# Moving the activation rows of a float32 encoder from 64 to 112 bytes past a multiple of 256

## The chip, the cores and the metric

The kernel runs on one core of a Trainium2 chip. The metric is the device time of one execution in microseconds (us), and the number compared is the median of several executions. Before the change three executions took 1151.05, 1151.22 and 1156.51 us.

## What is computed

The reference is a trunk of two encoder layers over 256 tokens of width 1024, all in float32. One layer is

```
h = x + 0.5 * swiglu(rms_norm(x), w_ffn1_in, w_ffn1_out)          # 1024 -> 2*2816 -> 1024
q, k, v, c, g = split(rms_norm(h) @ w_in)                         # 512, 128, 128, 1024, 2048 columns
y_attn = window_attention(norm(q), norm(k), v, sink, bias) @ w_attn_out
y_conv = silu(layer_norm(depthwise_conv(glu(c)))) @ w_conv_out    # 31 taps, 512 channels
h = h + (sigmoid(g_attn) * y_attn + sigmoid(g_conv) * y_conv) @ w_o
h = h + 0.5 * swiglu(rms_norm(h), w_ffn2_in, w_ffn2_out)
x = h + (p @ w_pe_proj) * sigmoid(rms_norm(h) @ w_pe_gate)
```

Some 200 MB of weights are read once, and each weight is used for 256 tokens.

## The kernel before

**Layout.** Activations lie transposed: 128 channels on the partitions, and along a partition one row of 256 tokens (1024 bytes) for each group of 128 channels. A product with a weight matrix loads a 128x128 block of weights into TensorE (512 bytes per partition) and moves one such row of 256 tokens past it.

**Three products for one.** To keep float32 accuracy with the type float32r, every operand is cut in two: a high part, which is the value cast to float32r, and a low part, which is the rest. `mm3` (lines 309 to 317) then issues three matmuls for each 128x128 block: high weights on high rows (L315), high weights on low rows (L316), low weights on high rows (L317). Each matmul has a weight load of its own.

**Weights.** `Weights` (lines 42 to 135) loads units of 1 MB through the queue of SP (L76) into four raw buffers. From these ScalarE makes the high part (L100) and VectorE the low part (L101), in seven buffers each of `w_hi` and `w_lo`, 4096 bytes per partition. A unit is loaded once a raw buffer is free, and prepared some tiles ahead of its use.

**Stages of a layer.** `ffn` (L545) computes the 22 hidden groups (`ps_gu`), cuts each hidden row into `h_hi` and `h_lo`, and multiplies those down (`ps_fo`). `mix` (L593) computes the two halves of the convolution's input (`ps_c`), keys and values (`ps_kv`), queries (`ps_q`), the gates (`ps_g`), then attention, the output products in plain float32 (`ps_ao`, `ps_co`), and `w_o` on the rows `ym` (`ps_wo`). A second `ffn` follows, and `embed` (`ps_pp`, `ps_pe`). The order of instructions on each engine is set by a planner that goes by priorities and by the costs of its own model.

**Roles.** In `mm3` the weights are loaded and the rows move. In `keys_values` (L666, matmuls L676 to L678) and `queries` (L710, L720 to L722) it is the other way round: a 128-token piece of a row is loaded, and the prepared weights move, 256 columns at a time for the keys and values and 512 for the queries.

**Where the buffers lie.** Pools are laid one after another along each partition in the order in which they are opened, and a pool's tiles one after another in it. In the program before, the prepared weight tiles begin at byte 64768 and follow each other at steps of 4096 bytes, all multiples of 256. Behind them `gap0` at byte 122112, a tile of 64 bytes that nothing reads, moves what follows: `x32` at 122176, the rows' high part at 130368 and low part at 138560, which is 64 bytes past a multiple of 256 each. A second such gap (`gap1`) and one at the start of `mix_pool` do the same for `h_hi`, `h_lo`, `xe`, `pT` and `ym`. So every row that moves in `mm3` begins 64 bytes past a multiple of 256 and every block of weights at a multiple of 256. These addresses are those of the built program.

Of the kernel before, what the change touches and what calls it, by code (L numbers as in the profile page):

```python
# [9 lines left out]
F32 = mybir.dt.float32  # L10
F32R = mybir.dt.float32r
# [4 lines left out]
P = 128  # L16
T = 256
D = 1024
KD = D // P
L = 2  # L20
FF = 2816
KF = FF // P
# [3 lines left out]
KC = CD // P  # L26
# [10 lines left out]
WEIGHTS_LAG = 100  # L37
ATTN = 7
W_BUFS = 7


class Weights:
# [96 lines left out]
def encoder_kernel(ctx: ExitStack, tc: tile.TileContext, a: dict, out: bass.AP):  # L139
    nc = tc.nc  # L140
# [3 lines left out]
    raw_pool = ctx.enter_context(tc.tile_pool(name="raw_pool", bufs=RAW_BUFS))  # L144
    w_pool = ctx.enter_context(tc.tile_pool(name="w_pool", bufs=W_BUFS))
    gap0 = ctx.enter_context(tc.tile_pool(name="gap0", bufs=1))
    xp = ctx.enter_context(tc.tile_pool(name="xp", bufs=1))
    tmp = ctx.enter_context(tc.tile_pool(name="tmp", bufs=2))
    gap1 = ctx.enter_context(tc.tile_pool(name="gap1", bufs=1))
    edge = const.tile([P, 24], F32, name="edge")  # L150
    nc.gpsimd.memset(edge, 0.0)
    for gap in (gap0, gap1):
        nc.gpsimd.memset(gap.tile([P, 16], F32, name="gap"), 0.0)
    dram = ctx.enter_context(tc.tile_pool(name="dram", bufs=1, space=bass.MemoryType.DRAM))
    mmp = ctx.enter_context(tc.tile_pool(name="mmp", bufs=4, space=PS))
    atp = ctx.enter_context(tc.tile_pool(name="atp", bufs=2, space=PS))
# [4 lines left out]
    def at_tile(name):  # L161
        return atp.tile([P, 1024], F32, name=name, tag="at")
# [7 lines left out]
    for i in range(4):  # L170
        s = slice(i * 256, (i + 1) * 256)
# [5 lines left out]
    def load_params(tile_, rows, load):  # L177
        r0 = 0
        for name in rows:
            if name in ("q_norm", "k_norm"):  # L180
                for hf in range(2):
                    load(tile_[r0 : r0 + L, hf * HD : (hf + 1) * HD], a[name])
                r0 += L
                continue
            n = a[name].shape[1] // P
            load(tile_[r0 : r0 + L * n, :], a[name].rearrange("l (k p) -> (l k) p", p=P))
            r0 += L * n
# [150 lines left out]

    x32 = xp.tile([P, KD, T], F32, name="x32", tag="x32")

    def new_x(tag, name):
        return (
            xp.tile([P, KD, T], F32R, name=name + "h", tag=tag + "h"),
            xp.tile([P, KD, T], F32R, name=name + "l", tag=tag + "l"),
        )

    pending = []

# [94 lines left out]
    def bcast(r, n):  # L443
        return r.unsqueeze(1).broadcast_to([P, n, T])
# [38 lines left out]
    late = {}  # L483

    rows_late = ("norm_mix", "norm_ffn2", "norm_pe", "conv_b", "conv_ln_g", "conv_ln_b", "q_norm", "k_norm")

    def late_loads(hp):
        def load(dst, src):
            tc.keep_in_program_order(nc.sync.dma_start(dst, src))

        rows = hp.tile([80, P], F32, name="rows_late")
        load_params(rows, rows_late, load)
        cw_ld = hp.tile([TAPS * KC, L, P], F32, name="cw_ld")
        for l in range(L):
            load(cw_ld[:, l, :], a["conv_w"][l].rearrange("t (c p) -> (t c) p", p=P))
        onehot = hp.tile([33, NREL], F32, name="onehot")
        load(onehot, a["onehot"])
        rb = const.tile([33, NH], F32, name="rb")
        nc.gpsimd.memset(rb[32:33, :], NEG)
        load(rb[0:32, :], a["rel_bias"])  # L500
        sink = const.tile([P, L * NH], F32, name="sink")
        load(sink, a["sink"].rearrange("l h -> (l h)").partition_broadcast(P))
        late["sink"] = sink
        late["ld"] = rows, cw_ld, onehot, rb

    def late_params():
        place_params(late["ld"][0], rows_late, n_par)

    def late_tables(hp):
        rows, cw_ld, onehot, rb = late.pop("ld")  # L510
        cw = const.tile([P, L, TAPS, KC], F32, name="cw")
        for l in range(L):
            ps = at_tile("ps_cw")
            nc.tensor.transpose(ps[:, : TAPS * KC], cw_ld[:, l, :], ident[: TAPS * KC, : TAPS * KC])
            nc.scalar.copy(out=cw[:, l].rearrange("p t c -> p (t c)"), in_=ps[:, : TAPS * KC])
        late["cw"] = cw

        kg = const.tile([P, L], F32, name="kg")
        cq, ck = col["q_norm"][0], col["k_norm"][0]
        nc.vector.scalar_tensor_tensor(  # L520
            out=kg, in0=par[:, cq : cq + L], scalar=HD ** -0.5, in1=par[:, ck : ck + L], op0=ALU.mult, op1=ALU.mult
        )
        late["kg"] = kg

        ps = at_tile("ps_rb")
        nc.tensor.matmul(ps[:NH, :NREL], rb, onehot, start=True, stop=True)
        tb = hp.tile([NH, NREL], F32, name="tb")
        nc.vector.tensor_copy(tb, ps[:NH, :NREL])
        late["tb"] = tb
# [13 lines left out]


    def ffn(hp, l, x_in, stat_in, gain_name, xn, stat, hooks):  # L545
        h = (
            hp.tile([P, KF, T], F32R, name="h_hi"),
            hp.tile([P, KF, T], F32R, name="h_lo"),
        )

        def gate_up(j):
            ps, products = pair("ps_gu", x_in, j == 0)

            def evac():
                gu = tmp.tile([P, 2, T], F32, name="gu")
                nc.vector.tensor_tensor(
                    out=gu, in0=ps, in1=bcast(stat_in.r, 2), op=ALU.mult
                )
                sg = tmp.tile([P, T], F32, name="sg")
                nc.scalar.activation(out=sg, in_=gu[:, 0, :], func=AF.Silu)  # L560
                hh = tmp.tile([P, T], F32, name="hh")
                nc.vector.tensor_tensor(out=hh, in0=sg, in1=gu[:, 1, :], op=ALU.mult)
                split((h[0][:, j, :], h[1][:, j, :]), hh)

            group(products, evac)

        def down(f):
            ps = mm_tile("ps_fo")

            def evac():  # L570
                nc.vector.scalar_tensor_tensor(
                    out=x32[:, f, :], in0=ps[:, :T], scalar=0.5, in1=x32[:, f, :], op0=ALU.mult, op1=ALU.add
                )
                emit_x(f, pcol(gain_name, l, f), xn, stat)

            group(
                [
                    lambda i=i, k0=k0: mm3(ps[:, :T], ws.get(), h, first=i == 0, last=i == 2, x_k0=k0)
                    for i, (k0, n) in enumerate(KGROUPS)
                ],  # L580
                evac,
            )

        for j in range(KF):
            if j in hooks:
                hooks[j]()
            gate_up(j)
        for f in range(KD):
            down(f)
        flush_urgent()  # L590


    def mix(l, u, st, xn, stat):  # L593
        cw, kg, bias, sink = (late[n] for n in ("cw", "kg", "bias", "sink"))
        with tc.tile_pool(name="mix_pool", bufs=1) as mp:
            nc.gpsimd.memset(mp.tile([P, 8], F32, name="gap"), 0.0)
            cpad = mp.tile([P, KC, T + 2 * PAD], F32, name="cpad", tag="cpad")
            nc.gpsimd.memset(cpad[:, :, 0:PAD], 0.0)
            nc.gpsimd.memset(cpad[:, :, PAD + T :], 0.0)
# [302 lines left out]
            for i in range(KC):  # L902
# [5 lines left out]
                if i == 0:  # L908
# [1 line left out]

            ym = [
                (
                    mp.tile([P, KC, T], F32R, name=f"ym_h{i}", tag="s", bufs=2),
                    mp.tile([P, KC, T], F32R, name=f"ym_l{i}", tag="pTs", bufs=2),
                )
                for i in range(2)
            ]
# [104 lines left out]

    def embed_input(hp):
        p_ld = late.pop("p_ld")
        pT = (hp.tile([P, 2, T], F32R, name="pT_h"), hp.tile([P, 2, T], F32R, name="pT_l"))
        ps = mm_tile("ps_pt")
        for e in range(2):
            for t in range(2):
                nc.tensor.transpose(
                    ps[:, e * T + t * P : e * T + (t + 1) * P], p_ld[:, t, e * P : (e + 1) * P], ident  # L1030
                )
        split(pT, ps.rearrange("p (e t) -> p e t", e=2))
        late["pT"] = pT

    st = r_cur
    for l in range(L):
        with tc.tile_pool(name="ffn1_pool", bufs=1) as hp:
            hooks = {1: lambda: late_loads(hp), 5: late_params, 6: lambda: late_tables(hp), 8: late_write, 12: late_bias} if l == 0 else {}
            xn, stat = new_x("xa", f"xm{l}"), Stat()
            ffn(hp, l, x_cur, st, "norm_mix", xn, stat, hooks)  # L1040
        x_cur, st = xn, stat.finish(3, tokens=True)
        xn, stat = new_x("xa", f"xf{l}"), Stat()
        mix(l, x_cur, st, xn, stat)
        x_cur, st = xn, stat.finish(3)
        with tc.tile_pool(name="ffn2_pool", bufs=1) as hp:
            xe = (hp.tile([P, KD, T], F32R, name="xe_h"), hp.tile([P, KD, T], F32R, name="xe_l"))
            stat = Stat()
            ffn(hp, l, x_cur, st, "norm_pe", xe, stat, {0: lambda: embed_load(l), 4: lambda: embed_input(hp)})
            x_cur, st = xe, stat.finish(4)
            xn, stat = (new_x("xa", f"xn{l}") if l + 1 < L else None), Stat()  # L1050
            embed(l, x_cur, st, xn, stat)
            x_cur, st = xn, stat.finish(3)
# [39 lines left out]
```

## Time and profile before

| | |
|---|---|
| three executions | 1151.05, 1151.22, 1156.51 us |
| profiled execution, first to last instruction (span) | 1155.8 us |
| TensorE matmuls (PE) busy | 1136.7 us, 98% of the span |
| TensorE weight loads (PEld) busy | 1100.9 us, 95% |
| VectorE (DVE) busy | 812.1 us, 70% |
| ScalarE (ACT) busy | 610.4 us, 53% |
| DMA | 203 MB, 176 GB/s on average |

For the profiled execution the span is the only time there is; it lies 4.6 us above the median of the three and 0.7 us below the longest of them. A matmul's duration in the profile, some 280 ns, is not its cost: matmuls follow each other in a pipeline, and what one costs is the distance from its start to the start of the next.

### The profile page before, as it was taken

To read this page: it belongs to the slowest core of one execution; us is meant where nothing else is said; L and a number is where in the kernel's file an instruction comes from. 1 tells how busy PE (TensorE), PEld (TensorE's weight loads), DVE (VectorE), ACT (ScalarE), POOL (GpSimd) and SP (SyncE) were. 2 spreads that over 40 slices of the span, in tenths; PEclk is the share of its full clock that TensorE was granted. 3 is DMA by queue.
4 is the path that set the end of the run, shared out by engine and by line. 5 is a ranking of instruction groups with operands and counts; after the bars stand their busy time and mean duration, and the time that the engine had idled before them with its cause. 6 is when DMAs were issued, how large, how long until landed. Compare 5 with 4: busy or idle time off the path is not lost.

```text
span 1155.8 us, 21813 instructions
## 1 busy us (share of the span) xinstructions
PE 1136.7 (98%) x9082; PEld 1100.9 (95%) x9082; DVE 812.1 (70%) x1214; ACT 610.4 (53%) x1029; POOL 88.8 (8%) x123
## 2 busy tenths in 40 slices
PE   7999999999989999999999999999999999999998
PEld 7999999998879999999999999999987899999997
DVE  5866656798767766656886666669986686666564
ACT  6644444676346544444664444457753564444443
POOL 3000001211002000001110000113000010000110
PEclk9999999999999999999999999999999999999999
DMA  8866556545074565546556464566522664644541
GB/s 256 265 236 213 170 176 208 182 149 138 8 254 157 187 215 168 179 166 219 188 177 204 162 207 156 171 218 197 143 77 65 227 228 152 214 163 149 200 147 37
DMA packets 195695, 203.00 MB, mean 176 GB/s; under 512 B 3731, under 2 KB 188899, under 8 KB 195596
## 3 DMA queue, kind: packets, MB, share of 16 engines
q1 hardware_dynamic: 195564, 201.60, 52.9%
q8 instruction: 71, 1.16, 0.4%
q14 instruction: 28, 0.23, 0.1%
q10 hardware_dynamic: 32, 0.01, 0.0%
HBM read 200.53 MB, written 1.06 MB: 174 GB/s over the span
## 4 chain that ended last, share of the span: by engine, by line
PE 95%; DMA 2%; DVE 2%; ACT 1%; issue 0%; SPq 0%; ACTq 0%; DVEq 0%
PE ps_gu L317 14%; PE ps_gu L315 14%; PE ps_gu L316 14%; PE ps_fo L315 7%; PE ps_fo L317 7%; PE ps_fo L316 7%; PE ps_g L315 3%; PE ps_g L317 3%; PE ps_g L316 3%; PE ps_ao L852 2%; DMA raw<-in_w_o_dram 2%; PE ps_s L760 1%; PE ps_wo L316 1%; PE ps_c L315 1%; PE ps_pe L317 1%; PE ps_c L317 1%
## 5 line engine op out<-in xcount | busy, mean ns | idle before, releaser
L101 DVE TENSOR_TENSOR w_lo<-raw,w_hi 128x1024 fp32r<-128x1024 f32 (+1 forms) x368 | 441.6, 1204 | 227.8 <-ACT w_hi L100 225.9
L100 ACT CAST w_hi<-raw 128x1024 fp32r<-128x1024 f32 (+1 forms) x368 | 377.8, 1032 | 411.6 <-PE ps_gu L316 207.5
L315 PE MATMUL ps_fo<-h_hi,w_hi 128*128 128x256 f32 x704 | 196.1, 279 | 0.0
L316 PE MATMUL ps_fo<-h_lo,w_hi 128*128 128x256 f32 x704 | 195.9, 279 | 0.0
L317 PE MATMUL ps_fo<-h_hi,w_lo 128*128 128x256 f32 x704 | 195.9, 279 | 0.0
L317 PEld LDWEIGHTS ps_fo<-h_hi,w_lo 128*128 128x128 f32 x704 | 131.8, 188 | 0.0
L315 PEld LDWEIGHTS ps_fo<-h_hi,w_hi 128*128 128x128 f32 x704 | 131.8, 188 | 0.0
L316 PEld LDWEIGHTS ps_fo<-h_lo,w_hi 128*128 128x128 f32 x704 | 131.7, 187 | 0.0
L404 POOL TENSOR_TENSOR sq_acc<-sq_acc,sq 128x256 f32<-128x256 f32 x56 | 56.9, 1015 | 887.0 <-ACT sq L403 886.5
L315 PE MATMUL ps_gu<-x0h,w_hi 128*128 128x256 f32 x352 | 99.4, 282 | 2.0 <-ACT x L460 2.0
L612 DVE SCALAR_TENSOR_TENSOR y<-cpad,cw,y 128x256 f32<-128x256 f32 x240 | 101.2, 477 | 0.1
L317 PE MATMUL ps_gu<-x0h,w_lo 128*128 128x256 f32 x352 | 99.4, 282 | 0.2 <-DVE w_lo L101 0.2
L316 PE MATMUL ps_gu<-x0l,w_hi 128*128 128x256 f32 x352 | 98.9, 281 | 0.0
L315 PE MATMUL ps_gu<-xf0h,w_hi 128*128 128x256 f32 x352 | 98.6, 280 | 0.0
L315 PE MATMUL ps_gu<-xf1h,w_hi 128*128 128x256 f32 x352 | 98.6, 280 | 0.0
L316 PE MATMUL ps_gu<-xn0l,w_hi 128*128 128x256 f32 x352 | 98.5, 280 | 0.0
L315 PE MATMUL ps_gu<-xn0h,w_hi 128*128 128x256 f32 x352 | 98.4, 280 | 0.0
L316 PE MATMUL ps_gu<-xf0l,w_hi 128*128 128x256 f32 x352 | 98.4, 280 | 0.0
L316 PE MATMUL ps_gu<-xf1l,w_hi 128*128 128x256 f32 x352 | 98.4, 280 | 0.0
L317 PE MATMUL ps_gu<-xf0h,w_lo 128*128 128x256 f32 x352 | 98.3, 279 | 0.0
L317 PE MATMUL ps_gu<-xf1h,w_lo 128*128 128x256 f32 x352 | 98.3, 279 | 0.0
L317 PE MATMUL ps_gu<-xn0h,w_lo 128*128 128x256 f32 x352 | 98.2, 279 | 0.0
(225 smaller groups left out, 2677.8 us busy)
## 6 DMA issues: line engine op xcount, KB each, us to landing
raw<-in_w_ffn_in_dram SPq DMA_DIRECT2D x86, 1024.0 KB
raw<-in_w_in_dram SPq DMA_DIRECT2D x30, 1024.0 KB
raw<-in_w_ffn_out_dram SPq DMA_DIRECT2D x32, 896.0 KB
raw<-in_w_ffn_out_dram SPq DMA_DIRECT2D x16, 1024.0 KB
raw<-in_w_o_dram SPq DMA_DIRECT2D x8, 1024.0 KB
raw<-in_w_pe_gate_dram SPq DMA_DIRECT2D x8, 1024.0 KB
raw<-in_w_attn_out_dram SPq DMA_DIRECT2D x8, 512.0 KB
raw<-in_w_conv_out_dram SPq DMA_DIRECT2D x4, 1024.0 KB
```

Source lines behind the costliest of these rows:

```text
L100: nc.scalar.copy(out=hv[:, :, d0 : d0 + w], in_=src),
L101: nc.vector.tensor_tensor(out=lv[:, :, d0 : d0 + w], in0=src, in1=hv[:, :, d0 : d0 + w].bitcast(F32), op=ALU.subtract,),
L315: nc.tensor.matmul(ps, wh[:, k0 + k, cols], xh[:, kx, :], start=f, stop=False)
L316: nc.tensor.matmul(ps, wh[:, k0 + k, cols], xl[:, kx, :], start=False, stop=False)
L317: nc.tensor.matmul(ps, wl[:, k0 + k, cols], xh[:, kx, :], start=False, stop=e)
L404: nc.gpsimd.tensor_tensor(out=self.acc, in0=self.acc, in1=sq, op=ALU.add)
L612: nc.vector.scalar_tensor_tensor(out=y[:, i, :], in0=src, scalar=w, in1=y[:, i, :], op0=ALU.mult, op1=ALU.add)
L760: nc.tensor.matmul(ps[:, c, :], qT[v * HD : (v + 1) * HD, c, qb * P : (qb + 1) * P], kT[v * HD : (v + 1) * HD, :], start=True, stop=True,)
L852: nc.tensor.matmul(ps[:, c * T : (c + 1) * T], w[:, k, c * P : (c + 1) * P], x[:, k, :], start=k == 0, stop=k == KC - 1,)
```

## The change

The helper `rows` makes every pair of activation rows that `mm3` moves: the tile is 256 bytes longer (`ROW`, 64 elements), and the rows begin 16 bytes into it (`PLACE`, 4 elements). The gap ahead of the rows' pool grows from 64 to 96 bytes (`G0`); the other two keep their sizes. So `x`, `h`, `ym`, `xe` and `pT` begin at 96 + 16 = 112 bytes past a multiple of 256, and the other tiles behind the first gap (`x32`, scratch, the convolution's input and output, attention's tiles) move from 64 to 96 past it, the convolution's input from 96 to 128. The prepared weights stay where they were. A variable that was called `rows` is renamed.

```diff
+ROW = 64
+G0, G1, G2 = 24, 16, 8
+PLACE = 4
...
-    for gap in (gap0, gap1):
-        nc.gpsimd.memset(gap.tile([P, 16], F32, name="gap"), 0.0)
+    for gap, n in ((gap0, G0), (gap1, G1)):
+        nc.gpsimd.memset(gap.tile([P, n], F32, name="gap"), 0.0)
...
+    def rows(pool, k, name, **kw):
+
+        t = pool.tile([P, k * T + ROW], F32R, name=name, **kw)
+        return t[:, PLACE : PLACE + k * T].rearrange("p (k t) -> p k t", t=T)
+
     def new_x(tag, name):
-        return (
-            xp.tile([P, KD, T], F32R, name=name + "h", tag=tag + "h"),
-            xp.tile([P, KD, T], F32R, name=name + "l", tag=tag + "l"),
-        )
+        return tuple(rows(xp, KD, name + part, tag=tag + part) for part in "hl")
...
-        h = (
-            hp.tile([P, KF, T], F32R, name="h_hi"),
-            hp.tile([P, KF, T], F32R, name="h_lo"),
-        )
+        h = tuple(rows(hp, KF, "h_" + part) for part in ("hi", "lo"))
...
-            nc.gpsimd.memset(mp.tile([P, 8], F32, name="gap"), 0.0)
+            nc.gpsimd.memset(mp.tile([P, G2], F32, name="gap"), 0.0)
...
-                    mp.tile([P, KC, T], F32R, name=f"ym_h{i}", tag="s", bufs=2),
-                    mp.tile([P, KC, T], F32R, name=f"ym_l{i}", tag="pTs", bufs=2),
+                    rows(mp, KC, f"ym_h{i}", tag="s", bufs=2),
+                    rows(mp, KC, f"ym_l{i}", tag="pTs", bufs=2),
...
-        pT = (hp.tile([P, 2, T], F32R, name="pT_h"), hp.tile([P, 2, T], F32R, name="pT_l"))
+        pT = tuple(rows(hp, 2, "pT_" + part) for part in "hl")
...
-            xe = (hp.tile([P, KD, T], F32R, name="xe_h"), hp.tile([P, KD, T], F32R, name="xe_l"))
+            xe = tuple(rows(hp, KD, "xe_" + part) for part in "hl")
```

More of the change, by code (lines that the diff above doesn't have):

```diff
@@ L489, in load @@
             tc.keep_in_program_order(nc.sync.dma_start(dst, src))
-        rows = hp.tile([80, P], F32, name="rows_late")
-        load_params(rows, rows_late, load)
+        row_ld = hp.tile([80, P], F32, name="rows_late")
+        load_params(row_ld, rows_late, load)
         cw_ld = hp.tile([TAPS * KC, L, P], F32, name="cw_ld")
@@ L503, in late_loads @@
         late["sink"] = sink
-        late["ld"] = rows, cw_ld, onehot, rb
+        late["ld"] = row_ld, cw_ld, onehot, rb
     def late_params():
@@ L509, in late_tables @@
     def late_tables(hp):
-        rows, cw_ld, onehot, rb = late.pop("ld")
+        _, cw_ld, onehot, rb = late.pop("ld")
         cw = const.tile([P, L, TAPS, KC], F32, name="cw")
```

## The prediction

> **What bounds the kernel now.** I read the profile's page first: the busy shares, the granted clock, and the shares of the chain of waits by engine.
>
> ```profile
> span 1155.8 us, 21813 instructions
> ...
> PE 1136.7 (98%) x9082; PEld 1100.9 (95%) x9082; DVE 812.1 (70%) x1214; ACT 610.4 (53%) x1029; POOL 88.8 (8%) x123
> ...
> PEclk9999999999999999999999999999999999999999
> ...
> PE 95%; DMA 2%; DVE 2%; ACT 1%; issue 0%; SPq 0%; ACTq 0%; DVEq 0%
> ```
>
> TensorE has work in hand for 98% of the span, at the full clock in every slice, and 95% of the chain that ended last is TensorE itself. Then the list of what TensorE waited for, longest and shortest entry:
>
> ```profile
> PE ps_yc L893 <- DVE yn L883: 3.7, 2, 1.9
> ...
> PE ps_gu L317 <- DVE w_lo L101: 0.2, 1, 0.2
> ```
>
> No entry is above 3.7 us. So the end is set by how closely matmuls follow each other. The groups of instructions by line give their number; one row of each group stands for its three lines (L315, L316, L317), which have the same count:
>
> ```profile
> L315 PE MATMUL ps_fo<-h_hi,w_hi 128*128 128x256 f32 x704 | 196.1, 279 | 0.0
> L315 PE MATMUL ps_gu<-x0h,w_hi 128*128 128x256 f32 x352 | 99.4, 282 | 2.0 <-ACT x L460 2.0
> L315 PE MATMUL ps_g<-xm0h,w_hi 128*128 128x256 f32 x128 | 36.8, 287 | 0.0
> L315 PE MATMUL ps_pe<-xe_h,w_hi 128*128 128x256 f32 x128 | 36.5, 286 | 0.0
> L315 PE MATMUL ps_wo<-ym_h,w_hi 128*128 128x256 f32 x128 | 35.1, 282 | 0.5 <-ACT ym_h L448 0.5
> L315 PE MATMUL ps_c<-xm0h,w_hi 128*128 128x256 f32 x64 | 18.0, 282 | 0.0
> L315 PE MATMUL ps_pp<-pT_h,w_hi 128*128 128x256 f32 x32 | 8.9, 280 | 0.0
> ```
>
> `ps_gu` has four such groups (x0, xn0, xf0, xf1), `ps_g` and `ps_c` two each (xm0, xm1). That is 3 x (704 + 4 x 352 + 2 x 128 + 128 + 128 + 2 x 64 + 32) = 3 x 2784 = 8352 matmuls whose moved operand the change moves, out of 9082 records. What one costs, from start to start, comes from stretches inside an `ffn`, in which they run alone; the columns are the stretch, its length, PE busy with its count, clock, DMA share and GB/s:
>
> ```profile
> 420.00:520.00 100.00, 100.00 (x851) 1.00 0.52 173
> 980.00:1080.00 100.00, 100.00 (x851) 1.00 0.55 182
> ```
>
> 100 us / 851 = 117.5 ns each, in layer 0 and in layer 1 alike. 8352 x 117.5 ns = 981 us: 85% of the span.
>
> **Is that all the matmul needs?** The change can gain only if part of the 117.5 ns hangs on where operands lie. The trace of before holds rows of the same shape with another placement. For the keys and values the roles are exchanged: the loaded block is a piece of a row (64 bytes past a multiple of 256), the moved one is prepared weights (at the multiple). For the queries too, with 512 moved columns. Columns of these rows: count, shortest/median/longest duration in ns, first to last start.
>
> ```profile
> L676 PEld LDWEIGHTS ps_kv<-w_hi,xm0h x16: 187/188/188, 213.9 to 219.0; 128*128 128x128 f32 x16
> L676 PE MATMUL ps_kv<-w_hi,xm0h x16: 276/276/283, 214.0 to 219.1; 128*128 128x256 f32 x16
> ...
> L676 PE MATMUL ps_kv<-w_hi,xm1h x16: 276/276/282, 780.7 to 785.8; 128*128 128x256 f32 x16
> ```
>
> ```profile
> L720 PE MATMUL ps_q<-w_hi,xm0h x16: 388/396/398, 219.5 to 230.0; 128*128 128x512 f32 x16
> L720 PE MATMUL ps_q<-w_hi,xm1h x16: 388/396/398, 786.2 to 796.7; 128*128 128x512 f32 x16
> ```
>
> Each line here is every third matmul, so from the first start to the last lie 15 x 3 = 45 distances. Keys and values: 5.1 us / 45 = 113.3 ns, in both layers. The same 128x128 load, the same 256 moved columns, the same type, 4.2 ns less; what differs is which operand lies 64 bytes on. Queries: 10.5 us / 45 = 233.3 ns for twice the columns. Two bounds for a stream that nothing disturbs come from the chain of waits in order of time (start, us, what): plain float32 matmuls, and transposes, which pass 128 columns at half speed.
>
> ```profile
> 273.72 0.87 PE ps_pt L797 x8
> ...
> 313.23 2.59 PE ps_ao L852 x12
> ```
>
> 0.87 us / 8 = 108.8 ns; 2.59 / 12 = 215.8 ns, which is twice 107.9. In time these stand for 256 and 512 columns at full speed. So a matmul of `mm3` runs 8.7 ns above the closest spacing that the trace shows for such a stream, one of the keys 4.5 ns above it, one of the queries 233.3 - 215.8 = 17.5 ns. I read this as two readers of the same memory, the moved rows and the next weight load, that get in each other's way by an amount that depends on their relative place. That is an inference: no row shows a collision itself.
>
> A rule of the Trainium skill speaks against it: "TensorE: Matmul & The Clock Gate", section "Step-by-step: what each phase is for", says that TensorE has two independent read ports to SBUF and that loading the next weights takes no bandwidth from the running matmul; by it the time would stay 1151 us. The rows of `ps_kv` and the 851-matmul stretches, 113.3 against 117.5 ns for one shape, do not fit that rule as it stands, though they don't show the cause.
>
> **The change part by part.**
>
> 1. *The 8352 moved rows go from 64 to 112 bytes past the weights' place.* The trace of before has no row at 112. Bounds: below, 108.8 ns (nothing left to gain beyond it), which is 8352 x 8.7 ns = 73 us; above, the loss that one weight load causes in the queries, 108.8 + 17.5 = 126.3 ns, which is 8352 x 8.8 = 73 us more. Between ends so far apart I take the row that is nearest in shape, the keys' 113.3 ns: 8352 x 4.2 ns = 35 us less. In it the moved operand lies at -64, that is 192, from the loaded one; 112 is not there, but it too has left 64, and I have no reason to put it nearer to the worse side. "TensorE: Matmul & The Clock Gate" of the Trainium skill, section "Back-to-back issue gap", gives N/2.4 + 2.5 ns for a matmul by itself, which is 109.2 ns for 256 columns; the estimate by that page is 8352 x 8.3 ns = 69 us less.
>
> 2. *Keys, values and queries* now load at 112 and move at 0: 2 x 48 matmuls each. At worst they gain or lose what they stand above the bound, 96 x 4.5 + 96 x 17.5 ns = 2.1 us. I count 0. The plain float32 products (`ps_ao`, `ps_co`) already run at 215.8 ns, which is the bound, and their rows only move from 64 to 96: 0.
>
> 3. *ScalarE and VectorE write rows at 112 instead of 64.* The nearest rows: L627 writes the convolution's input 156 bytes past a multiple of 256, L449 writes rows at 64.
>
> ```profile
> L627 DVE TENSOR_TENSOR cpad<-sg,gu x8: 419/424/442, 217.0 to 815.4; 128x256 f32<-128x256 f32 x8
> ...
> L449 DVE TENSOR_TENSOR h_lo<-hh,h_hi x88: 417/419/427, 42.8 to 1062.2; 128x256 fp32r<-128x256 f32 x88
> ...
> L448 ACT CAST h_hi<-hh x88: 393/402/408, 41.6 to 1061.0; 128x256 fp32r<-128x256 f32 x88
> ```
>
> 424 against 419 ns: place costs VectorE at most 1%. For ScalarE there is no such row; were its casts (402 ns in the third row) twice as long, the 8 ends of stages at which TensorE may wait for the last row would each lose 0.4 us, 3 us in all. I take 0, since VectorE shows nothing.
>
> 4. *The longer tiles and the larger gap* cost one memset that clears 32 bytes more, and no instruction is added in any loop. The tiles fit: the second `ffn`'s pool ends 160 bytes below the partition's end. 0.
>
> **Does the supply keep up?** A faster TensorE asks sooner for weights. The stages (columns: stretch, length, then PE, PEld, DVE, ACT and POOL busy with counts, clock, DMA share, GB/s):
>
> ```profile
> 14.00:207.00 193.00, 192.97 (x1626) 191.86 (x1626) 128.86 (x158) 98.47 (x143) 14.33 (x17) 1.00 0.65 216
> ...
> 344.00:559.00 215.00, 215.00 (x1825) 214.89 (x1824) 145.06 (x182) 109.05 (x160) 14.43 (x14) 1.00 0.56 187
> ...
> 887.00:910.00 23.00, 19.58 (x95) 16.75 (x94) 15.17 (x20) 11.71 (x15) 0.00 (x0) 1.00 0.71 244
> ```
>
> In an `ffn` a unit of 1 MB (1.05 million bytes) feeds 48 matmuls: 186 GB/s at 117.5 ns, 193 at 113.3, 201 at 108.8. The first `ffn` was served at 216 GB/s and the end of `mix` at 244. VectorE is busy 67% of an `ffn` and would be at 70%. Neither becomes the bound. At the end of `mix` TensorE does wait, and the chain lies on loads of `w_o`:
>
> ```profile
> 893.06 8.35 DMA raw<-in_w_o_dram
> ```
>
> These start when TensorE frees a raw buffer, so they move forward with it and keep their length. The gain of 35 us is not eaten there; it is also not made there.
>
> **Sum.** 1155.8 - 35 = 1121 us of span. The profiled execution lies 4.6 us above the median, so against the median it is 1151.2 - 35 = **1116 us**.
>
> **The rivals.**
>
> - *All of the excess goes* (from 117.5 to some 109 ns): 1151 - 73 = 1078 us. For it: spacing of 108.8 exists. Against it: no row with a 188 ns float32r load shows it.
> - *A small part goes* (1 to 2 ns, 8 to 17 us): some 1139 us. For it: 112 is only 48 bytes from the old place, while the keys' row lies 128 bytes off it.
> - *Nothing changes*: the moved rows and the weight load don't disturb each other, and the keys' lower spacing comes from what is loaded and what moves, not from where it lies. 1151 us. For it: no row shows two places with the same roles. Against it: equal shapes and types, 4.2 ns apart. The Trainium skill's rule of two independent ports ("TensorE: Matmul & The Clock Gate", "Step-by-step: what each phase is for") is this case.
> - *The new place is worse*: at 112 the two readers meet more often. The point from which it decides is a spacing above 118.2 ns (0.5%, 6 us). Half of the way to the bound of 126.3 ns is 121.9 ns, 37 us more: 1188 us. For it: the queries show that one load can cost a matmul 17.5 ns, twice what it costs now, so 64 is not the worst place. Against it: the keys.
> - *The change does not do what it says*: the addresses, added up from the pools' order and sizes, are 112 past a multiple of 256 for all rows of the diff, since each new tile is a multiple of 256 long. I give it nothing.
>
> **How the numbers follow.** The forecast, a spacing of 111.3 to 115.4 ns (1099 to 1134 us), 0.45; all of it 0.13; a small part 0.13; nothing 0.14; worse 0.15. A measurement of this kernel tells about 0.5% from no change, 6 us. Faster: 0.45 + 0.13 + 0.13 = 0.71; within: 0.14; slower: 0.15. For 8 in 10 the range takes in the forecast, the small part, nothing (to 1157 us) and most of the way to the lower bound (1080 us); it leaves out the worse case and the last of the lower one. The forecast's own range is 1099 to 1134 us.
>
> **What would show it.** In the stretch 420 to 520 us the count of matmuls should be 100 us / 113.3 ns = 883 instead of 851, with the same in every `mm3` group, durations of VectorE and ScalarE unchanged, and TensorE's waits still a few us. A count near 851 would say that the place does not matter; one above 900 that the whole excess was the place; fewer than 846 that 112 is worse. If the spacing falls and the span does not, TensorE's idle time on `w_hi`, `w_lo` or the raw loads must have grown, and the part on the supply is wrong. If high and low rows differ from each other, a multiple of 256 is not the right measure of place, since the two now differ by 256 bytes in their place past a multiple of 512.

## The result and the profile after

The changed kernel takes 1124.15 us (median of 4 executions, 1122.83 to 1124.70) against 1151.13 us before (4 executions, 1150.66 to 1156.51), 27 us less. The quotient of these medians is 0.977; the recorded ratio is 0.974, 95% interval 0.9706 to 0.9774. In a later comparison it took 1124.19 us against 1156.26 us (recorded ratio 0.9732, 0.9691 to 0.9773). The forecast was 1116 us, with 1080 to 1157 as the range.

The page of the profiled execution after the change, which took 1124.69 us, with the lines that answer to those of before:

```profile
span 1122.9 us, 21813 instructions
...
PE 1103.5 (98%) x9082; PEld 1067.8 (95%) x9082; DVE 811.9 (72%) x1214; ACT 611.2 (54%) x1029; POOL 89.5 (8%) x123
...
PEclk9999999999999999999999999999999999999999
...
PE 91%; DMA 5%; DVE 2%; ACT 1%; issue 0%; ACTq 0%; DVEq 0%
```

The same number of instructions on each engine, and the same busy time on VectorE, ScalarE and GpSimd within 1 us. The span fell by 32.9 us and TensorE's busy time by 33.2 us: everything came from the spacing of matmuls, nothing from waits, which add up to 15.6 us after and 15.2 us before. Matmuls in the two stretches of `ffn` that the prediction used (columns as there):

```profile
420.00:520.00 100.00, 100.00 (x885) 1.00 0.53 180
980.00:1080.00 100.00, 100.00 (x884) 1.00 0.57 194
```

885 in place of 851, that is 113.0 ns each; worked out from the starts themselves, the mean distance in each 20 us of these stretches is 113.33 to 113.34 ns after, and 117.77 to 117.78 before. Some of what TensorE waited for, the longest two entries and the one on prepared weights (total, times, longest):

```profile
PE ps_par L199 <- DMA rows_first<-in_norm_ffn_dram: 4.0, 1, 4.0
PE ps_yc L895 <- DVE yn L885: 3.7, 2, 1.9
...
PE ps_gu L320 <- DVE w_lo L104: 0.5, 1, 0.5
```

The supply keeps up: 0.5 us of waiting for prepared weights in the first `ffn`, where it was 0.2. The larger DMA share in the chain of waits (5%, was 2%) lies in the first 50 us, where the chain now runs through loads of weights. TensorE's list shows no wait for weights beyond these 0.5 us.

The writers of the rows, now at 112:

```profile
L454 DVE TENSOR_TENSOR h_lo<-hh,h_hi x88: 416/418/429, 42.7 to 1032.2; 128x256 fp32r<-128x256 f32 x88
```

```profile
L453 ACT CAST h_hi<-hh x88: 392/398/410, 41.4 to 1031.1; 128x256 fp32r<-128x256 f32 x88
```

418 against 419 ns and 398 against 402 ns: VectorE and ScalarE do not care.

### The profile page after: what moved, and what is told of

Its sections match the earlier page's. It is cut to its first block, busy times and chain, and to the rows that moved or that the text cites. A ratio compares the mean times of both kernels' runs of the same rounds, so it can differ in the third digit from the quotient of the medians.

```text
span 1122.9 us, 21813 instructions
## 1 busy us (share of the span) xinstructions
PE 1103.5 (98%) x9082; PEld 1067.8 (95%) x9082; DVE 811.9 (72%) x1214; ACT 611.2 (54%) x1029; POOL 89.5 (8%) x123
## 4 chain that ended last, share of the span: by engine, by line
PE 91%; DMA 5%; DVE 2%; ACT 1%; issue 0%; ACTq 0%; DVEq 0%
PE ps_gu L319 13%; PE ps_gu L318 13%; PE ps_gu L320 13%; PE ps_fo L319 7%; PE ps_fo L318 7%; PE ps_fo L320 7%; PE ps_g L318 3%; PE ps_g L320 3%; PE ps_g L319 3%; DMA raw<-in_w_ffn_in_dram 2%; PE ps_ao L854 2%; DMA raw<-in_w_o_dram 2%; PE ps_s L762 1%; PE ps_wo L319 1%; PE ps_o L809 1%; PE ps_c L318 1%
## 5 line engine op out<-in xcount | busy, mean ns | idle before, releaser
L319 PE MATMUL ps_fo<-h_lo,w_hi 128*128 128x256 f32 x704 | 193.2, 275 | 0.0
L320 PE MATMUL ps_fo<-h_hi,w_lo 128*128 128x256 f32 x704 | 193.2, 275 | 0.0
L318 PE MATMUL ps_fo<-h_hi,w_hi 128*128 128x256 f32 x704 | 193.2, 275 | 0.0
```

The source lines that it names most:

```text
L318: nc.tensor.matmul(ps, wh[:, k0 + k, cols], xh[:, kx, :], start=f, stop=False)
L319: nc.tensor.matmul(ps, wh[:, k0 + k, cols], xl[:, kx, :], start=False, stop=False)
L320: nc.tensor.matmul(ps, wl[:, k0 + k, cols], xh[:, kx, :], start=False, stop=e)
```

## The experiments

The prediction left three things open: whether place is the cause at all, what kind of place (distance from the weights, or the row's own), and whether two readers that disturb each other are the reason. The experiments are variants of the whole kernel and three kernels that do nothing but run streams of matmuls (and copy `x` to the output), one stream for each pair of places, each behind a plain float32 matmul. In these the steady spacing is the mean of the last 30 to 40 distances from start to start in the trace.

### Streams at many places (first sweep)

The loop of the first sweep (`...` stands for lines left out, comments added):

```
for name, ws, off, n, m, reps in CONFIGS:      # ws: shift of the loaded blocks, off: place of the rows, bytes
    brk()                                      # one plain float32 matmul
    ...
    for i in range(reps):
        k = i % 8
        wk = ws // 4 + 128 * k
        xk = off // 4 + (n * k if n <= 256 else n * (k % 4))
        ... nc.tensor.matmul(ps[0:m, 0:n], w[:, wk : wk + m], x[:, xk : xk + n], start=i == 0, stop=i == reps - 1)
```

> This kernel computes nothing of the reference: it copies x to the output and runs streams of float32r matmuls (128x128 loaded, 256 moved, 96 in a row unless said), each behind one plain float32 matmul. The name of a stream gives the distance in bytes by which the moved rows lie past a multiple of 256 and, with s, by how much the loaded blocks are shifted too. Theory A (the distance between moved row and loaded block, taken modulo 256, sets the spacing): 117.8 ns at 64, 113.3 at 112 and at 192, about 120 at 144; streams with both shifted by 48, 64, 128 or 192 bytes have the spacing of the unshifted ones; 320, 368, 576 and 624 repeat 64 and 112. Rival B (the place of the moved row itself counts): the shifted streams differ from the unshifted ones. Rival C (only a multiple of 512 or 1024 counts): 320 differs from 64, or 576 does. If a smaller loaded block (32 or 64 columns) still shows 117 ns at 64, the weight load is not the second reader.

Four streams in order of time (start, length in us, count):

```profile
111.76 11.55 PE L121 MATMUL m64r<-x,w 128*128 128x256 f32 x96
...
181.99 11.16 PE L121 MATMUL m112r<-x,w 128*128 128x256 f32 x96
...
543.00 11.61 PE L121 MATMUL s48m112r<-x,w 128*128 128x256 f32 x96
...
577.84 11.16 PE L121 MATMUL s64m112r<-x,w 128*128 128x256 f32 x96
```

Steady spacing in ns, loaded blocks at a multiple of 256:

```
row at    0     16     32     48     64     80     96    112
       120.0  116.7  116.7  118.4  117.8  120.0  120.0  113.3
row at  128    144    160    176    192    208    224    240
       118.7  116.7  118.7  119.2  117.8  119.2  118.4  117.1
row at  320    368    576    624        (256 + 64, 256 + 112, 512 + 64, 512 + 112)
       117.8  113.3  117.8  113.3
both shifted by       48     64    128    192
 distance 64       118.3  117.8  117.8  117.8
 distance 112      118.3  113.3  113.4  113.3
fewer loaded columns     row at 0     64    112
 64 loaded                113.3  116.7  116.7
 32 loaded                120.0  116.7  113.3
```

So the streams by themselves show both numbers of the kernel, 117.8 at 64 and 113.3 at 112, and of the sixteen places 112 alone is at 113.3. Place modulo 256 is enough (rival C falls). Shifting both by a multiple of 64 changes nothing (rival B falls), but a shift of both by 48 does, so theory A, the distance alone, falls too. 192 gave 117.8, where 113.3 was expected; 144 gave 116.7, where 120 was. With 64 loaded columns the order of the places changes: 0 is the best there, and 112 is no longer at 113.3. At 64 both narrower loads still leave 116.7 ns, which by the sign stated beforehand (about 117 at 64) speaks against the weight load as the second reader. With 512 moved columns 144 and 192 take 233.3 ns, which is also what the queries took, whose moved operand lies 192 past the loaded one.

### Rows at 144, 192 and 96 in the whole kernel

```diff
-PLACE = 4
+PLACE = 12        # 144;  24 for 192, 0 for 96
```

> The changed kernel with the rows at 144 instead of 112 bytes past a multiple of 256. Theory A: the keys' and values' matmuls of the changed kernel stand at a distance of 0 - 112, that is 144 modulo 256, and take 120.2 ns on average, so mm3 takes about 120 ns and the time is 1124 + 8352 x 6.6 ns = 1179 us; the keys then stand at 0 - 144 = 112 and fall to 113.3 ns. Rival (the keys' rise came with the exchange of roles, and any place other than 64 is good for mm3): 113.3 ns, 1124 us.

> The changed kernel with the rows at 192. Theory A: the keys of the kernel before stood at 0 - 64 = 192 and took 113.3 ns, so mm3 takes 113.3 ns and the time is 1124 us as at 112; the keys then stand at 0 - 192 = 64 and take 117.8 ns. Rival (112 itself is a good place and not a good distance): between 117 and 120 ns, 1150 to 1180 us.

> The changed kernel without the 16 bytes ahead of the rows: the larger gap alone, rows at 96. From the first sweep (119.95 ns at 96): mm3 at 120 ns, 8352 x 2.2 ns = 18 us above the kernel before. Rival (leaving 64 is what helped, 112 is nothing special): as fast as at 112, 32 us below the kernel before.

| rows at | time, us | against before on the same chip | steady spacing of `mm3` |
|---|---|---|---|
| 96 | 1175.5 | 1.0176 (1.012 to 1.0232) | 120.0 ns |
| 112 | 1124.2 | 0.9732 (0.9691 to 0.9773) | 113.3 ns |
| 144 | 1160.6 | 1.0028 (1.0009 to 1.0047) | 118.7 ns in every `ffn` |
| 192 | 1141.0 | 0.9878 (0.9773 to 0.9983) | 113.3 and 117.8 ns |

(96 and 192 are two executions each, 144 eight.) The larger gap alone, that is the change without its 16 bytes, loses 19 us: leaving 64 was not what helped, and since every other tile lies as in the changed kernel, the 16 bytes of the rows make the whole difference between the two. 96 came as expected. 144 and 192 came out between what theory A and its rival gave, and both fail there; the keys of the kernel with rows at 144 took 118.4 ns, where theory A gave 113.3. In the kernel with rows at 192, three stretches of three `ffn`s:

```profile
60.00:160.00 100.00, 100.00 (x851) 1.00 0.59 199
420.00:520.00 100.00, 100.00 (x851) 1.00 0.53 177
600.00:700.00 100.00, 100.00 (x885) 1.00 0.55 188
```

One placement, two spacings in one execution. Each lasts: from about 60 us on it is 117.8 ns for 140 us, from 560 us on 113.3 ns for 200 us. A place need not have one price.

### The kernel before, profiled again

> The kernel before, unchanged, to see what lies between its profiled execution (span 1155.8 us) and its median of 1151 us. If the spacing in mm3 varies from execution to execution, some stretch of it shows less than 117.8 ns; if not, TensorE's waits differ, or the span is 1155 us again.

> The kernel before a third time, to catch one of its executions of 1148 to 1151 us with a profile. If it is one, some 1000 to 1500 matmuls of mm3 follow each other at 113.3 instead of 117.8 ns (5 to 7 us); if it is one of 1156 us, every stretch shows 117.8 as in the two profiles so far.

The second profile (1156.16 us) shows 117.8 ns in every `ffn`, as the first did. The third is of an execution of 1151.57 us:

```profile
100.00:200.00 100.00, 100.00 (x884) 1.00 0.59 196
...
600.00:700.00 100.00, 100.00 (x851) 1.00 0.54 179
```

Against the first profile of the same kernel:

```profile
100.00:200.00 100.00, 100.00 (x851) 1.00 0.57 189
600.00:700.00 100.00, 100.00 (x851) 1.00 0.54 178
```

From about 50 to 206 us this execution ran at 113.33 ns, and after that at 117.8 again. 155 us / 113.33 ns = 1370 matmuls at 4.45 ns less are 6.1 us, which is the difference between its span of 1149.8 us and that of 1155.8 us. So the rows at 64 have both spacings as well, and the fast one is hit now and then: of the nine executions that shared a chip with the kernels at 144 and 192, two took 1150.1 and 1151.1 us and seven 1156.8 to 1158.4. Why an execution falls into the one or the other is not known.

### Pairs of places at four bytes' distance (second sweep)

```diff
+    ('w0m0r', 0, 0, 256, 128, 72),
+    ('w0m4r', 0, 4, 256, 128, 72),
...
```

> Again only streams of matmuls and a copy of x to the output, nothing else of the reference: loaded blocks at 0, 4, 8, 16, 32 and 48 bytes past a multiple of 256 (w), moved rows at every fourth byte from 0 to 252 (m), 72 matmuls each. Theory A2 (the spacing hangs on the distance modulo 256 and on the loaded block's place modulo 64): loaded at 0 and moved at 112 gives 113.3 ns; loaded at 48 and moved at 192, the case of the keys in the changed kernel, about 120; loaded at 16 and moved at 128, the case of the keys with rows at 144, about 118.4; with loaded at 32 and moved at 144 the distance is 112, but the place modulo 64 differs, so it is not bound to be 113.3. Rival (the distance alone): every pair at a distance of 112 gives 113.3 ns. If 113.3 ns (136 ticks of 1.2 GHz) is a floor of this shape, no stream is below it; a stream near 109 ns would say that the excess can go altogether.

Loaded blocks at 0, 4, 8, 16, 32 and 48, rows at 64 places each, 384 streams. Steady spacing (ns) and number of streams, rounded to whole ns:

```
113: 7   116: 1   117: 15   118: 85   119: 46   120: 105   121: 45   122: 49   123: 29   124: 2
at 113.3 (loaded, moved): (0,112) (4,80) (8,48) (16,208) (32,144) (32,224) (48,240)
distance 112:             (0,112) 113.3  (4,116) 122.5  (8,120) 121.6  (16,128) 120.0  (32,144) 113.3  (48,160) 120.0
the keys' cases:          (48,192) 120.0   (16,128) 120.0
```

The distance alone does not set the spacing; the pair does. 113.33 ns is the least of all 384, and seven streams reach it. The changed kernel is at this least spacing. Each pair ran once here, and a pair can have several spacings, so a higher figure need not be a pair's only one. The keys of the changed kernel, whose loaded block lies at 112, which is 48 modulo 64, take 120.2 ns on average, and the stream for their case 120.0. With rows at 144 the keys took 118.4 ns, which theory A2 gave for the stream too; the stream took 120.0. Whether that pair has both spacings was not tried.

### Which stream loses the time (third sweep)

The lines in which it differs from the first sweep (shortened, comments added):

```
lw, mx = (wb, xb) if kind == "bf16" else (w, x)                 # bf: both operands in bfloat16
...
    kw, kx = k if "w" in moves else 0, k if "x" in moves else 0 # onlyx: always the same loaded block
```

> Streams of matmuls alone again, nothing else of the reference but a copy of x to the output; o is the place of the moved rows, loaded blocks at 0. Which stream loses the time? Theory L (the next weight load disturbs the moved rows): the loss over the closest spacing is one per weight load, so it does not grow with the moved columns (n64 to n512), it shrinks with fewer loaded columns (c128 to c1), and it is gone where every matmul loads the same block (onlyx). Theory M (the moved float32r stream itself runs slower than one column per 2.4 GHz tick, by an amount that its start fixes): the loss grows in proportion with the moved columns (8.7 ns for 256 and 17.5 for 512 at one place) and stays with one loaded column. Under M bf16 rows, half as wide, are free of it: 109 ns for 256 columns at every place; under L they lose too. Rep streams repeat one place behind 1 to 4 plain float32 matmuls: if a place has one steady spacing, all 16 of a place agree; if several, 192 shows both 113.3 and 117.8 ns, and 64 may too, which would explain the executions of 1148 to 1151 us of the kernel before.

Lengths of some streams (start, length in us):

```profile
107.07 8.88 PE L212 MATMUL n256o0r<-x,w 128*128 128x256 f32 x72
115.93 8.72 PE L212 MATMUL n256o64r<-x,w 128*128 128x256 f32 x72
124.63 8.46 PE L212 MATMUL n256o112r<-x,w 128*128 128x256 f32 x72
...
354.68 8.43 PE L212 MATMUL c64n256o0r<-x,w 128*64 128x256 f32 x72
...
371.71 8.64 PE L212 MATMUL c64n256o112r<-x,w 128*64 128x256 f32 x72
...
658.80 8.88 PE L212 MATMUL c1n256o0r<-x,w 128*1 128x256 f32 x72
...
676.28 8.43 PE L212 MATMUL c1n256o112r<-x,w 128*1 128x256 f32 x72
...
732.05 8.02 PE L212 MATMUL bf256o0r<-xb,wb 128*128 128x256 bf16 x72
740.14 8.02 PE L212 MATMUL bf256o64r<-xb,wb 128*128 128x256 bf16 x72
748.22 8.02 PE L212 MATMUL bf256o112r<-xb,wb 128*128 128x256 bf16 x72
```

Steady spacing in ns with rows at 0, 64, 112, loaded blocks at 0:

```
                                  0      64     112
float32r, 512 moved columns   226.7   228.8   231.0
float32r, 384                 173.3   173.3   173.3
float32r, 256                 120.0   117.8   113.3
float32r, 192                 111.7   111.7   111.7
float32r, 128                 111.7   111.7   111.7
float32r, 256, 64 loaded col. 113.3   116.7   116.7
float32r, 256, 32 loaded col. 113.3   113.3   113.3
float32r, 256, 16 loaded col. 120.0   116.7   113.3
float32r, 256, 8 loaded col.  116.7   113.3   113.3
float32r, 256, 1 loaded col.  120.0   116.7   113.3
float32r, 256, always the same block and row
                              120.0   117.8   113.3
bfloat16, 512                 215.8   215.8   215.8
bfloat16, 256                 109.2   109.2   109.2
plain float32, 256            215.8 (for each of a matmul's two parts)
```

The size of the weight load does not set the loss. With one loaded column instead of 128, or with the same block every time, the loss over the 109.2 ns of bfloat16 is still there and depends on the place. Between 1 and 128 loaded columns it goes up and down without a trend, and what is best at one width is not at another: 0 at 64 columns, 112 at 128. With 32 loaded columns all three places are at 113.3, while in the first sweep they were at 120.0, 116.7 and 113.3, so here too one pair has several spacings. Of theory L's signs the second and the third fail outright (the loss does not shrink with the load, and it is not gone with one block); the first, a loss that does not grow with the moved columns, holds at 0 and fails at 64 and 112 (next paragraph). What this does not settle is a loss that every weight load makes, whatever its size: each of these streams has a load before every matmul, and no stream ran without.

Theory M, a moved float32r stream that is itself slower by an amount that its start fixes, fits only in part. The loss does not grow in proportion with the moved columns: from 256 to 512 it goes from 10.8 to 10.8 ns at 0, from 8.6 to 13.0 at 64 and from 4.2 to 15.1 at 112. Nor does the row's start alone fix the amount, since the loaded block's place (the second sweep, the shift by 48) and its width both change the spacing. The bfloat16 streams lose nothing at the three places tried. In them both operands are half as wide, and a weight load takes 98 ns on average where the float32r loads of 128 columns take about 190, so they do not tell which operand frees them. By what mechanism place acts stays open. For 512 columns and 128 loaded ones 0 is the best and 112 the worst of the three, so a place that is good for one length is not for another. (The streams of 64 moved columns are left out: from 190 to 228 us of this run the granted clock was 0.50, and their spacing went from 112 to 213 ns.)

The repeated streams, 16 for each place, loaded blocks at 0, differing in how many plain matmuls (1 to 4) and how many of their own went before:

```
rows at  64:  2 of 16 at 113.3, 14 at 117.8
rows at 112: 16 of 16 reach 113.3 (the four shortest within the last 30 to 40: 113.5 to 113.8 on average)
rows at 144:  6 of 16 at 116.7, 10 at 118.7
rows at 192:  8 of 16 at 113.3,  8 at 117.8
```

This agrees with the kernels: 64 mostly ends at 117.8 ns, 192 as often at the one as at the other, and 112 at 113.3 in all 16.

### The changed kernel elsewhere

> The changed kernel on the chip on which the kernel before took 1156.8 us in most executions. If the executions of 1151 us of the kernel before are the exception, the difference is 8326 x 4.1 ns = 34 us, a ratio of 0.971; if the changed kernel varies with the chip in the same way, it is 1129 us here and the ratio stays at 0.976.

1124.19 us against 1156.26 us, span 1121.4 us, with 884 and 885 matmuls in stretches of 100 us: all its executions on record lie between 1122.8 and 1124.7 us. The kernel before varies, in that the fast spacing is hit more or less often; whether by chip or by chance is not shown.

```diff
+    gapw = ctx.enter_context(tc.tile_pool(name="gapw", bufs=1))
+    nc.gpsimd.memset(gapw.tile([P, 16], F32, name="gap"), 0.0)     # 8 for 32 bytes
     w_pool = ctx.enter_context(tc.tile_pool(name="w_pool", bufs=W_BUFS))
```

> The changed kernel with a gap of 64 bytes ahead of the weight tiles, so that weights begin at 64 and rows at 176 past a multiple of 256, the distance 112 kept. By the shifted streams of the first sweep (113.3 ns at s64, s128 and s192) the steady spacing is 113.3 ns and the time 1124 us, as without the gap. Rival (the weights have to begin at a multiple of 256): above 117 ns, 1155 us or more.

> The same with a gap of 32 bytes: weights at 32, rows at 144, distance 112. The second sweep shows 113.3 ns for this pair in one stream; a single stream does not tell whether the pair always ends there. If always, 1124 us; if it is a pair with two steady spacings, part of mm3 runs at 116.7 to 118.7 ns and the time lies between 1130 and 1160 us.

1124.09 us with weights at 64 and rows at 176, 1123.67 us with weights at 32 and rows at 144 (before, on that chip: 1157.1 us; ratios 0.9716, 0.9688 to 0.9744, and 0.9712, 0.9684 to 0.9741). So the weights need not begin at a multiple of 256; rows at 144, poor beside weights at 0, are good beside weights at 32. The expected 1124 us came in both, and neither differs from the changed kernel, since all three run at 113.3 ns, the least spacing seen.

## Why the prediction was right, and where it was not

- **Spacing sets the end.** Right: 33.2 us of TensorE's busy time gone, 32.9 us of span.
- **Step 1, the size.** The step took 113.3 ns from the keys' rows and got 113.33. The prediction's 117.5 ns, from a count in 100 us, was 0.3 ns low: from start to start it is 117.78. The distances below 150 ns between two matmuls of 256 moved columns add up to 980.0 us before (8331 of them) and 946.0 us after (8326): 34 us less, against 35 in the prediction. At the steady 4.45 ns they would be 37 us less. Of the 3 us between, some 2.5 are what follows a break in the stream and 0.6 are the keys'. After a transpose, a plain float32 matmul or another break the spacing is mostly 115 to 121 ns for up to some 15 matmuls, most often 10, before it settles (columns: start, length, instruction):

```profile
1101.36 0.38 PE L1003 MATMUL ps_out<-ident,x 128*128 128x128 f32 x2
1101.50 0.37 PE L318 MATMUL ps_pe<-xe_h,w_hi 128*128 128x256 f32 x1
...
1102.06 0.28 PE L319 MATMUL ps_pe<-xe_l,w_hi 128*128 128x256 f32 x1
1102.18 0.28 PE L320 MATMUL ps_pe<-xe_h,w_lo 128*128 128x256 f32 x1
...
1103.12 0.28 PE L319 MATMUL ps_pe<-xe_l,w_hi 128*128 128x256 f32 x1
1103.23 0.28 PE L320 MATMUL ps_pe<-xe_h,w_lo 128*128 128x256 f32 x1
```

  0.12 us apart at 1102.1, 0.11 at 1103.2.
- **The choice of the keys' row** was right in its number and by luck in its place. In place it stands for rows at 192, and 192 turned out to have two spacings, of which the keys showed the better one. 144, also away from 64, would have left the time within 0.3%, and 96 would have lost 1.8%. The prediction saw no reason to put 112 nearer to the worse side; it had no reason to put it nearer to the better one either. Of 384 pairs seven are at 113.3.
- **The inference of two readers** is what the runs do not bear out: the loss follows neither the size of the weight load nor its being a new block. That a load disturbs the moved rows by its mere presence is not refuted, since no stream ran without loads, and it is not shown. So the prediction's "loss that one weight load causes in the queries", its upper bound, is a figure of a place: the bare stream of 512 columns at 192 has the queries' 233.3 ns. That the operands' places decide, and that 4.2 ns of the 8.7 were to be had, did not depend on the inference.
- **The rival "all of the excess"** fails: 113.33 ns was the least in every float32r stream of 256 columns.
- **Step 2** was right as a sum and wrong in its parts: the keys rose to 120.2 ns, the queries stayed at 233.3 ns. The keys' cost is 96 x 6.5 ns = 0.6 us. The step's bound for a loss, what they stood above the closest spacing (4.5 ns each), was too small for them: nothing keeps a matmul from losing more than it had to gain.

One of the keys' three lines after; 5.4 us / 45 = 120.0 ns:

```profile
L678 PE MATMUL ps_kv<-w_hi,xm0h x16: 277/284/291, 207.9 to 213.3; 128*128 128x256 f32 x16
```

- **Steps 3 and 4 and the supply**: right, as the rows of the first section show.
- **The sum against the median** is the term that was mis-sized, by 6 of the 8 us between 1116 and 1124 (the other 2 are in the span, 1122.9 us against 1121): the profiled execution of before was set 4.6 us above the median and the gain taken off the median, but the two differ in the very thing that the change takes away. Three of those first four executions took about 1151 us, and one such execution, profiled later, had 155 us at 113.3 ns; I infer that those did too. From the profiled execution (span 1155.8) the change takes 32.9 us, from such an execution 27.
- **The rival that nothing changes** falls: 113.3 and 117.8 ns stand for equal streams at two places. The Trainium skill's two independent read ports ("TensorE: Matmul & The Clock Gate", "Step-by-step: what each phase is for") would give it. Whether a weight load takes anything from the running matmul, which that section denies, these runs leave open.
- **The lower bound.** The closest spacing of 108.8 ns, from transposes, is near what 256 columns take in bfloat16, 109.17 ns. The Trainium skill's N/2.4 + 2.5 ns ("TensorE: Matmul & The Clock Gate", "Back-to-back issue gap"), by estimate 109.2 ns for 256 columns, agrees with these bfloat16 streams, and with no float32r stream.

## What to carry to other kernels

In these streams a float32r matmul with 256 moved columns ran 4% to 13% above the 109.2 ns of bfloat16, by where in SBUF (the on-chip memory of the operands) both its operands begin, to a few bytes. Look at the distance from start to start in the trace, not at a duration, and sweep places in a kernel of bare streams, with the kernel's own sizes of load and row, since the order of places changes with both. Repeat each stream behind different breaks: a place is good only if it always settles at the low spacing. And where executions of one kernel differ by a fixed half per cent, compare matmul counts in equal stretches before a difference of medians is put down to a change.

## What the runs showed of the hardware

- Float32r streams of 256 moved columns settled at 113.3 to 123.5 ns over 384 pairs of places, seven of them at 113.3 and the next at 115.5; bfloat16 at 109.2 ns at the three places tried.
- One pair of places can have two steady spacings (64: 113.3 and 117.8 ns; 144: 116.7 and 118.7; 192: 113.3 and 117.8), each of which holds, here for up to 200 us, until something breaks the stream.
- After a break the stream at 112 took up to some 15 matmuls to settle in the kernel, most often 10, and 10 or 11 in the repeated streams.
- With 128 or 192 moved columns float32r streams stand at 111.7 ns at all three places, where bfloat16 with 128 columns takes 55.8 ns; what binds there was not tried.
- The number of loaded columns changes which place is best (64 loaded: 113.3 ns at 0 and 116.7 at 112; 128 loaded: 120.0 and 113.3), without a trend from 1 to 128.
